# Packing the own tiles of exponents in a sparse-attention layer

## The chip, the cores and the metric

The kernel runs on one core of a Trainium2 chip. The metric is the device time of one execution in microseconds (us); the median of three runs before the change is 1934.23 us. About 0.2% (3.9 us) is what a measurement of this kernel can tell from no change.

## The reference

Two layers act on 1024 tokens of width 1024. Layer 0 mixes with gated linear attention, layer 1 with sparse attention of 16 heads: an indexer scores all earlier keys, the 256 best are kept for each query, and softmax runs over these. The change touches layer 1 alone. What is computed there, for one head:

```
logits = einsum('bthd,btjd->bthj', q_b, k_sel) * ATTN_SCALE
logits = where(valid, logits, -inf)          # valid: idx <= t_pos
probs  = softmax(logits)                     # over the selected keys
o      = einsum('bthj,btjd->bthd', probs, v_sel)
out    = (o * silu(z)) @ w_out
```

The kernel does not gather: it adds a bias to the scores of all earlier keys, which hides those that were not selected, takes exponents, and multiplies by all values of earlier keys. One key and one value serve all 16 heads.

## The kernel before, in words

Layer 1 is done in two halves of 512 queries. Half 0 has four tiles of 128 keys, half 1 eight: four "past" ones, which every query may see, and four "own" ones, of which query tile t sees the first t+1. Ten of the sixteen own pairs of key tile and query tile are thus unmasked or on the diagonal, and six are empty.

For one head h of a half (function `attend`):

- `A(t)` (four steps, one for each query tile): TensorE (PE) forms the scores into tile `S`; VectorE (DVE) adds the bias, scales, and takes the row minimum `mx` (L1592, tile `P`); then `exp` on ScalarE (ACT, L1599) writes exponents to `sq` with one instruction and the row sum to `sm`; then `turned` (L1605) turns every 32x32 square of `sq` in place on DVE.
- `store` (L1618): four DMAs for each group of four key tiles write `sq` to a scratch tensor `sqd` in DRAM, with all sixteen places of key tile and query tile. Half 1 has two such groups: group 0 holds the past keys, group 1 the own keys. `load` (L1628) reads a group back with keys on the partitions: tile `PT`, 1 MB. In this text PT0 is the tile of group 0 and PT1 that of group 1. Half 0 has group 0 alone, in two buffers; half 1 has one buffer each for PT0 and PT1.
- `parts` (L1645 on ACT, L1643 on DVE) splits each key tile of `PT` into a high part `ph` and a low part, which takes the place in `PT`. `pv` multiplies by the values: three matmuls (L58, tile `o`) for each key tile, of which the third reads the low part; the last own key tile is used whole.
- `inverse` and `to_all` turn the row sums into a factor for the output, by way of a small DRAM row (`row`, then `inv`).

There is one buffer `sq` for all heads. So `exp` of the next head waits until the stores of this one have landed, and the store waits for the last `turned`.

The order of work on each engine is written by the program, with a clock of its own (`Flow.now`) that counts matmul columns alone. A step is put on a heap with a due time (`fl.at`) and is emitted when the clock has passed it and its conditions (`fl.req`) hold. Engines then run their lists in that order, each waiting for what it needs. All DMAs of this stage but the small `row` ones are issued from the SP queue, in order, and SP waits at a DMA whose inputs or buffers are not ready: those behind it wait too. Beside stores and loads these are the weights (`whi` and `wlo`, L174, 512 KB each).

Around the heads runs a fixed plan (`slots`): while one head's exponents are made, the head before is multiplied, and matmul units of projections (tile `pb`) fill the rest. Heads 0 to 3 have two units each; from head 4 on a slot has three. The emptied `P` buffers, `ph` (three) and the PSUM tiles bound how far ahead engines may run.

Of the kernel before, what the change touches and what calls it, by code (L numbers as in the profile page):

```python
# [10 lines left out]
F32 = mybir.dt.float32  # L11
# [12 lines left out]
HT = 512  # L24
# [253 lines left out]
def trunk_kernel(ctx, tc, x_tok, x_T, p_T, pos, freq, g_q, g_k, g_v, g_z, g_a, g_a2, g_ba, g_gn, g_o,  # L278
# [1276 lines left out]
    def attend(st, h, half, ap, sq):  # L1555
# [15 lines left out]
        def A(t):  # L1571
            def f():
                T = base + t
                n = 128 * T + 128
                (qh, ql), = get(("q", h))
                i = t % (half + 2)
                last = max(range(i, 4, half + 2))
                fl.req(("P", h, t - half - 2) in st if t != i else h == 0 or ("P", h - 1, last) in st)
                st["A", h] = t
                ts_ = slice(t * 128, t * 128 + 128)  # L1580
                P = ap.tile([128, 128 * (base + last) + 128], F32, tag=f"P{i}", name="P")[:, :n]
                if t == 0:
                    st["sm", h] = cp.tile([128, 4], F32, tag=("ss", "rs")[h % 2], name="sm", bufs=2)
                    st["mx", h] = cp.tile([128, 3, 8], F32, tag="mid", name="mx", bufs=2)
                sm, mx = st["sm", h], st["mx", h][:, 0, t:t + 1]
                lim = 3.0e38
                for a, e in cuts(n):
                    e2 = max(e, 256)
                    ps = spsum()
                    for i, (l, r) in enumerate(((qh, kT[0]), (qh, kT[1]), (ql, kT[0]))):  # L1590
                        mm(ps[:, :e2], l[:, ts_], r[:, a:a + e2], i == 0, i == 2)
                    dve.tensor_tensor_reduce(P[:, a:a + e], ps[:, :e], bias_t[T][:, a:a + e], op0=OP.add, op1=OP.min,  # L1592
                                             scale=-ATTN_SCALE, scalar=lim, accum_out=mx)
                    lim = mx

                def exp():
                    fl.req(st["x"] == nb * h)
                    to, rows = by_key[:, t, :n // 128], P.rearrange("p (j b r) -> p j b r", b=4, r=32)
                    act.activation(to, rows, AF.Exp, scale=-1.0, bias=mx, accum_out=sm[:, t:t + 1])  # L1599
                    st["P", h, t] = True  # L1600
                    after(0.4 + n / 1000.0, turned)

                def turned():
                    x = squares[:, t, :, :n // 128]
                    dve.transpose(x, x)  # L1605
                    st["D", h, t] = True
                after(0.9, exp)
            return f

        def store(i):  # L1610

            def f():
                get(*(("D", h, t) for t in range(4)))
                fl.req(st["x"] == nb * h + i)
                dt = st["dram", h, i] = dp.tile([4, 32, 4, HT], F32, tag=f"sq{i}", name="sqd", bufs=2)
                sq4 = sq.rearrange("p (b i c) -> p i b c", b=4, i=nb)
                for a in range(4):
                    nc.sync.dma_start(dt[:, :, a].rearrange("b p c -> p b c"), sq4[32 * a:32 * a + 32, i])  # L1618
                st["x"] += 1
            return f  # L1620

        def load(i):

            def f():
                dt, _ = get(("dram", h, i), ("dram", h, nb - 1))
                fl.req(st["pv"] >= (h * G - (0 if i else G - 4) if half else (h - 1) * G))
                PT = ap.tile([128, 4, HT], F32R, tag=f"PT{i}", name="PT", bufs=2 - half)
                nc.sync.dma_start(PT.bitcast(F32), dt.rearrange("b p a c -> (b p) a c"))  # L1628
                st["PT", h, i] = PT
            return f  # L1630

        def parts(g):
            def f():
                j, t0 = groups[g]
                PT, = get(("PT", h, j // 4))
                fl.req(st["sp"] - st["pv"] < 3)
                st["sp"] += 1
                lo = PT.rearrange("p a (j c) -> p j a c", c=128)[:, j % 4, :, 32 * t0:]
                ph = ap.tile([128, HT], F32R, tag="ph", name="ph", bufs=3)
                hi = ph[:, :HT - 128 * t0].rearrange("p (a c) -> p a c", a=4)  # L1640

                def second():
                    dve.tensor_sub(lo, lo.bitcast(F32), hi.bitcast(F32))  # L1643
                    st["parts", h, g] = hi, lo
                chain((0, lambda: act.activation(hi, lo.bitcast(F32), AF.Copy)), (0.8, second))  # L1645
            return f
# [39 lines left out]
        def pv(g):  # L1686
            first, last = g == 0, g == len(groups) - 1

            def f():
                (ph, pl), = get(("parts", h, g))  # L1690
                fl.req(not first or st.get("done", -1) == h - 1, not last or h < 5 or st["out"] >= h - 4)
                st["pv"] += 1
                if first:
                    st["o", h] = pp.tile([128, HT], F32, tag="o", name="o")
                o = st["o", h]
                o3 = o.rearrange("p (a c) -> p a c", c=128)
                j, t0 = groups[g]
                if last:
                    PT, = get(("PT", h, half))
                    whole = PT.bitcast(F32).rearrange("p a (j c) -> p j a c", c=128)[:, 3, :, 96:]  # L1700
                    mm(o3[:, :, 96:], vT[0][:, base + 3].bitcast(F32), whole, False, False)
                for i, (l, r) in enumerate(((vT[0], ph), (vT[1], ph), (vT[0], pl))):
                    mm(o3[:, :, 32 * t0:], l[:, j], r, first and i == 0, last and i == 2)
# [19 lines left out]

        n = range(len(groups))
        return [fl.ordered(x) for x in ([A(t) for t in range(4)], [parts(g) for g in n], [pv(g) for g in n],
                                     [store(i) for i in range(nb)], [load(i) for i in range(nb)], [inverse, to_all])]

    def dsa_out(st, js, ch, y, norm=None, ahead=1):
        fl.need(lambda: st.get("y") == NK)
# [86 lines left out]
    for half in range(NH):  # L1816
# [4 lines left out]
            nc.sync.dma_start(vT[0][:, 3].bitcast(F32), kv_s[4, :, 384:512])  # L1821
            nc.sync.dma_start(vT[0][:, 7].bitcast(F32), vf_s[1])
        fl.run(*(unit(u) for u in first_units))
        sq = ap.tile([128, (4 * half + 4) * HT], F32, name="sq")
        pool.memset(sq, 0.0)
        st["x"] = st["sp"] = st["pv"] = st["out"] = 0
        core = 8.6 if half else 3.6
        plan = list(slots())
# [1 line left out]
        for h, units in enumerate(plan, -1):  # L1830
# [5 lines left out]
            if h >= 0:  # L1836
# [16 lines left out]
            if h < 15:  # L1853
# [117 lines left out]
```

## Time and profile before

| what | value |
|---|---|
| runs, us | 1932.59, 1935.04, 1934.23; median 1934.23 |
| the profiled execution, us | 1935.94, with a span of 1934.2 |
| granted TensorE clock | 1.00 |
| PE, DVE, ACT busy | 99%, 77%, 52% of the span |
| half 0 of layer 1's heads | about 1070 to 1400 us of the span |
| half 1 of layer 1's heads | about 1470 to 1865 us |
| SP store and load issues | `sqd<-sq` 192 of 256 KB, `PT<-sqd` 48 of 1024 KB |

Times in the trace count from the span's start. A row of a timeline gives start, duration, engine, line, operation, output and input, shape, count, and in brackets how long the engine had been idle and what ended that. A row of the chain of waits gives start, duration and what ran. The stretches of a window table give, for each engine, the busy time and (x) the instructions, then the clock, the share of the DMA engines that was busy and GB/s. In DMA rows "SPq" is the SP queue issuing; its duration is that of issuing, not of the transfer.

### The profile page before, as it was taken

The numbers are of one execution on the slowest core, as the hardware profiler recorded it, in microseconds if no ns is written. First come the engines' busy times: TensorE is split into PE (matmuls) and PEld (weight loads), VectorE is DVE, ScalarE is ACT, GpSimd is POOL, SyncE is SP. The second block draws the span as 40 slices with busy tenths as digits, with TensorE's granted clock in tenths as the row PEclk, the third lists the DMA queues.
The fourth block names the chain that finished last, engine by engine and source line by source line (L and its number), as shares of the span: only waits on it lengthen the run. The fifth ranks groups of instructions, "written<-read, shape, count | busy, mean of one in ns | idle before, by whom it ended". The sixth has DMA issues, their size and how long they took to land.

```text
span 1934.2 us, 26875 instructions
## 1 busy us (share of the span) xinstructions
PE 1914.7 (99%) x8826; PEld 1590.6 (82%) x8826; DVE 1495.4 (77%) x3081; ACT 1002.4 (52%) x1896; POOL 153.0 (8%) x301
## 2 busy tenths in 40 slices
PE   9999999999999999999999999999999999999999
PEld 7888888888888888888888888888888778888887
DVE  5777666696778888878858987778798887777873
ACT  5564636445564646464535676756443443434432
POOL 0000000010010101010101001221001010000000
PEclk9999999999999999999999999999999999999999
DMA  4567766768667767677688588987877898888874
GB/s 156 207 218 230 225 220 215 225 207 274 223 221 262 244 224 247 222 242 228 211 287 302 169 294 288 318 293 283 305 247 283 324 305 302 299 303 289 290 285 142
DMA packets 200764, 488.91 MB, mean 253 GB/s; under 512 B 26504, under 2 KB 42928, under 8 KB 194480
## 3 DMA queue, kind: packets, MB, share of 16 engines
q1 hardware_dynamic: 193200, 474.55, 72.1%
q0 software_dynamic: 7424, 12.64, 2.0%
q8 instruction: 69, 1.13, 0.2%
q14 instruction: 71, 0.58, 0.1%
HBM read 343.18 MB, written 143.92 MB: 252 GB/s over the span
## 4 chain that ended last, share of the span: by engine, by line
PE 88%; DVE 5%; ACT 3%; DMA 2%; issue 1%; SPq 0%; DVEq 0%; ACTq 0%
PE pb L58 67%; PE o L58 8%; PE U L58 6%; PE S L58 5%; DMA PT<-sqd 1%; PE tr L58 1%; DVE sq L1605 1%; DVE PT L1643 0%; DMA wst<-in_g_v 0%; DVE sc L1141 0%; PE xt L62 0%; DVE wlo L191 0%; PE ix L58 0%; SPq L1618 0%; PE S L62 0%
## 5 line engine op out<-in xcount | busy, mean ns | idle before, releaser
L58 PE MATMUL pb<-x,whi 128*128 128x512 f32 x2272 | 704.2, 391 | 0.8 <-DVE x L411 0.7
L58 PEld LDWEIGHTS pb<-x,whi 128*128 128x128 f32 x2272 | 419.5, 188 | 80.0 <-DVE x L411 1.9
L58 PE MATMUL pb<-x,wlo 128*128 128x512 f32 x1136 | 442.6, 390 | 0.0
L58 PE MATMUL pb<-whi,u 128*128 128x512 f32 x1024 | 339.5, 392 | 1.5 <-ACT u L419 0.8
L58 PEld LDWEIGHTS pb<-x,wlo 128*128 128x128 f32 x1136 | 213.2, 188 | 45.8 <-DVE wlo L191 0.4
L58 PEld LDWEIGHTS pb<-whi,u 128*128 128x128 f32 x1024 | 192.2, 188 | 41.3 <-ACT u L419 1.2
L58 PE MATMUL pb<-wlo,u 128*128 128x512 f32 x512 | 199.6, 390 | 0.0
L191 DVE TENSOR_TENSOR wlo<-wst,whi 128x512 fp32r<-128x512 f32 x232 | 154.5, 683 | 35.1 <-ACT whi L189 34.9
L189 ACT ACTIVATE whi<-wst 128x512 fp32r<-128x512 f32 x232 | 136.4, 622 | 73.9 <-DMA wst<-in_g_k 28.8
L1599 ACT ACTIVATE sq<-P,mx 128x128 f32<-128x128 f32 (+7 forms) x128 | 98.8, 772 | 87.6 <-DVE mx L1592 58.0
L58 PE MATMUL S<-kT,q 128*128 128x512 f32 (+2 forms) x576 | 123.6, 343 | 1.7 <-DVE q L411 1.2
L1645 ACT ACTIVATE ph<-PT 128x512 fp32r<-128x512 f32 (+2 forms) x160 | 86.2, 558 | 63.0 <-PE o L58 43.4
L58 PEld LDWEIGHTS S<-kT,q 128*128 128x128 f32 x576 | 100.4, 188 | 20.5 <-DVE mx L1592 2.1
L58 PEld LDWEIGHTS pb<-wlo,u 128*128 128x128 f32 x512 | 96.2, 188 | 18.2
L1643 DVE TENSOR_TENSOR PT<-PT,ph 128x512 fp32r<-128x512 f32 (+2 forms) x160 | 92.6, 592 | 21.4 <-ACT ph L1645 21.2
L1207 ACT ACTIVATE tk<-sc,tki 128x768 f16<-128x768 f32 (+2 forms) x90 | 92.9, 1033 | 25.4 <-DVE tki L1216 21.6
L1605 DVE STREAM_TRANSPOSE sq<-sq 128x128 f32<-128x128 f32 (+7 forms) x128 | 97.7, 768 | 2.0 <-ACT sq L1599 2.0
L237 DVE TENSOR_TENSOR pst<-pst,phi 128x512 fp32r<-128x512 f32 x130 | 88.7, 682 | 7.4 <-ACT phi L233 7.4
L753 ACT ACTIVATE junk<-o 128x512 bf16<-128x512 f32 x32 | 19.1, 597 | 139.7 <-DVE ot L748 116.6
L58 PE MATMUL o<-ph,vT 128*128 128x512 f32 (+2 forms) x320 | 90.8, 365 | 0.0
L58 PE MATMUL pb<-whi,x 128*128 128x512 f32 x256 | 85.3, 392 | 0.0
L58 PE MATMUL U<-whi,x 128*128 128x512 f32 x256 | 84.6, 389 | 0.0
(330 smaller groups left out, 3400.4 us busy)
## 6 DMA issues: line engine op xcount, KB each, us to landing
whi<-whs SPq DMA_DIRECT2D x128, 512.0 KB, 6.1
wlo<-wls SPq DMA_DIRECT2D x128, 512.0 KB, 6.7
sqd<-sq SPq DMA_DIRECT2D x192, 256.0 KB, 4.4
PT<-sqd SPq DMA_DIRECT2D x48, 1024.0 KB, 7.7
whs<-phi SPq DMA_DIRECT2D x130, 256.0 KB, 4.1
wls<-pst SPq DMA_DIRECT2D x130, 256.0 KB, 4.1
wst<-in_g_z SPq DMA_DIRECT2D x32, 512.0 KB, 4.7
wst<-in_g_o SPq DMA_DIRECT2D x32, 512.0 KB, 5.1
```

Source lines behind the costliest of these rows:

```text
L58: self.pe.matmul(out, lhsT, rhs, start=start, stop=stop)
L189: self.nc.scalar.activation(hi[:, c], st[:, c], AF.Copy, scale=1.0 if gain is None else gain)
L191: self.nc.vector.tensor_sub(lo[:, c], st[:, c], hi[:, c].bitcast(F32))
L237: self.nc.vector.tensor_sub(st, st.bitcast(F32), hi.bitcast(F32))
L753: act.activation(junk, ps, AF.Square, accum_out=u["ss"][:, c:c + 1])
L1207: act.activation(junk()[:, :n], scs[j], AF.Sign, bias=cand[:, j:j + 1].bitcast(F32), accum_out=cnt[:, j:j + 1])
L1599: act.activation(to, rows, AF.Exp, scale=-1.0, bias=mx, accum_out=sm[:, t:t + 1])
L1605: dve.transpose(x, x)
L1643: dve.tensor_sub(lo, lo.bitcast(F32), hi.bitcast(F32))
L1645: chain((0, lambda: act.activation(hi, lo.bitcast(F32), AF.Copy)), (0.8, second))
```

## The change

- `exp` writes own key tiles to ten packed cells of 32 columns (times four for the key's quarter) and past key tiles to a separate region. So one instruction becomes one to three: for half 0 five a head where there were four, for half 1 nine.
- `turned` turns whole packed regions: in half 0 after query tiles 2 and 3; in half 1 the past region after tiles 1 and 3, half of it each time, the own region after 2 and 3.
- Own stores carry 320 columns, where they carried 512 (160 KB for 256 KB a DMA), and own loads 640 KB where they were 1024 KB. Past ones stay.
- In half 1, PT1 (own) has two buffers and is loaded as soon as it is stored, ahead of PT0 in the list of loads; it used to be loaded after the previous head's multiplication had ended.
- `sq` shrinks and is no longer zeroed (POOL's memset goes); row sums go to a wider tile, and one or two small additions bring the pieces of a sum together.
- `parts` and `pv` address the own tiles as runs of 32 columns. Matmul count, order and sizes stay.

```diff
+        cells = ((0, 1, 0),), ((0, 2, 2),), ((0, 2, 4), (2, 3, 1)), ((0, 4, 6),)
                 def exp():
-                    to, rows = by_key[:, t, :n // 128], P.rearrange("p (j b r) -> p j b r", b=4, r=32)
-                    act.activation(to, rows, AF.Exp, scale=-1.0, bias=mx, accum_out=sm[:, t:t + 1])
+                    rows = P.rearrange("p (j b r) -> p j b r", b=4, r=32)
+                    to = [(cell[:, c:c + e - j], rows[:, base + j:base + e], 8 if j else 0) for j, e, c in cells[t]]
+                    if half:
+                        to.append((past[:, t], rows[:, 0:base], 4))
+                    for x, r, i in to:
+                        act.activation(x, r, AF.Exp, scale=-1.0, bias=mx, accum_out=sm[:, i + t:i + t + 1])
                 def turned():
-                    x = squares[:, t, :, :n // 128]
-                    dve.transpose(x, x)
+                    get(*(("P", h, i) for i in range(t)))
+                    if half and t % 2:
+                        x = by_b[:, :, 0:HT].rearrange("p b (j x) -> p b j x", j=4)[..., 32 * t - 32:32 * t + 32]
+                        dve.transpose(x, x)
+                    if t > 1:
+                        x = by_b[:, :, HT * half:][:, :, 192 * (t - 2):192 + 128 * (t - 2)]
+                        dve.transpose(x, x)
...
+                n = HT if i < half else 320
+                dt = st["dram", h, i] = dp.tile([4, 32, 4, n], F32, tag=f"sq{n}", name="sqd", bufs=2)
...
-                fl.req(st["pv"] >= (h * G - (0 if i else G - 4) if half else (h - 1) * G))
-                PT = ap.tile([128, 4, HT], F32R, tag=f"PT{i}", name="PT", bufs=2 - half)
+                fl.req(st["pv"] >= (h * G - G + 4 if i < half else (h - 1) * G))
+                if i < half:
+                    PT = ap.tile([128, 4, HT], F32R, tag="PT0", name="PT")
+                elif half:
+                    PT = ap.tile([128, 4, 320], F32R, tag="PT1", name="PT", bufs=2)
...
+            if half:
+                dve.tensor_add(sm[:, 0:4], sm[:, 0:4], sm[:, 4:8])
+            dve.tensor_add(sm[:, 2:3], sm[:, 2:3], sm[:, 10:11])
...
-                                     [store(i) for i in range(nb)], [load(i) for i in range(nb)], [inverse, to_all])]
+                                     [store(i) for i in range(nb)], [load(i) for i in reversed(range(nb))],
...
-        sq = ap.tile([128, (4 * half + 4) * HT], F32, name="sq")
-        pool.memset(sq, 0.0)
+        sq = ap.tile([128, 4 * (HT * half + 320)], F32, name="sq")
...
-                    fl.at(start + 1.5, loads[1])
...
-                    fl.at(start + (max(dur - 1.0, 18.0) if h >= 0 else 16.0), loads[0])
+                    fl.at(start + (16.5 if h >= 0 else 15.0), loads[0])
+                    fl.at(start + (max(dur - 1.0, 18.0) if h >= 0 else 16.0), loads[1])
```

In the program after the change `loads[0]` is the load of PT1 and `loads[1]` that of PT0.

The SP queue of half 1 at the stores and loads of head 1, and the stores of head 2 with their loads, before (512 columns are a full group; `128x2048` is a whole PT tile):

```order
L1618 DMA sqd<-sq 32x4x512 x8
L1628 DMA PT<-sqd 128x2048 x2
L1676 DMA row<-uf 4x128
L174 DMA whi<-whs 128x1024
L174 DMA wlo<-wls 128x1024
L1684 DMA inv<-row 128x512
L1618 DMA sqd<-sq 32x4x512 x8
L174 DMA whi<-whs 128x1024
L174 DMA wlo<-wls 128x1024
L1628 DMA PT<-sqd 128x2048
```

The same place after the change (`128x1280` is the packed PT1):

```order
L1629 DMA sqd<-sq 32x4x512 x4
L1629 DMA sqd<-sq 32x4x320 x4
L1646 DMA PT<-sqd 128x1280
L1646 DMA PT<-sqd 128x2048
L1704 DMA row<-uf 4x128
L174 DMA whi<-whs 128x1024
L174 DMA wlo<-wls 128x1024
L1712 DMA inv<-row 128x512
L1629 DMA sqd<-sq 32x4x512 x4
L1629 DMA sqd<-sq 32x4x320 x4
L174 DMA whi<-whs 128x1024
L174 DMA wlo<-wls 128x1024
```

PT1 now stands between the last own store, whose data it reads, and PT0; before, PT0 came directly behind the stores (or behind the weights that follow them), and PT1 after it.

The DVE list of half 1 from the last transpose ahead of head 2's first split on, before (`PT<-PT,ph` is the split's second step for one key tile; the last transpose, `128x32x32`, is the one that the stores wait for):

```order
L1605 STREAM_TRANSPOSE sq<-sq 128x4x6x32
L1643 TENSOR_TENSOR PT<-PT,ph 128x4x128
L411 TENSOR_TENSOR q<-qf,q 128x512
L1605 STREAM_TRANSPOSE sq<-sq 128x4x7x32
L1643 TENSOR_TENSOR PT<-PT,ph 128x4x128
L1605 STREAM_TRANSPOSE sq<-sq 128x32x32
L1643 TENSOR_TENSOR PT<-PT,ph 128x4x128
L1528 SCALAR_TENSOR_TENSOR z<-z,pb 128x512
L1659 RECIPROCAL inverse_10144<-sm 128x4
```

The same place after the change:

```order
L1613 STREAM_TRANSPOSE sq<-sq 128x4x4x64
L1666 TENSOR_TENSOR PT<-PT,ph 128x4x128
L411 TENSOR_TENSOR q<-qf,q 128x512
L1616 STREAM_TRANSPOSE sq<-sq 128x4x192
L1666 TENSOR_TENSOR PT<-PT,ph 128x4x128
L1613 STREAM_TRANSPOSE sq<-sq 128x4x4x64
L1616 STREAM_TRANSPOSE sq<-sq 128x4x128
L1666 TENSOR_TENSOR PT<-PT,ph 128x4x128
L1528 SCALAR_TENSOR_TENSOR z<-z,pb 128x512
L1679 TENSOR_TENSOR mx<-mx 128x4
L1680 TENSOR_TENSOR mx<-mx 128x1
L1687 RECIPROCAL inverse_10144<-mx 128x4
```

After the first split there stood transposes of 896 and 1024 elements a row; now there are 768, 1024 (the past stores wait for this one) and 512 (the own stores). Two small additions stand ahead of the reciprocal.

More of the change, by code (lines that the diff above doesn't have):

```diff
@@ L1563, in attend @@
         G, nb = len(groups), half + 1
-        by_key = sq.rearrange("p (b j t r) -> p t j b r", b=4, t=4, r=32)
-        squares = sq.rearrange("p (b j t r) -> p t b j r", b=4, t=4, r=32)
+        by_b = sq.rearrange("p (b c) -> p b c", b=4)
+        past = by_b[:, :, 0:HT].rearrange("p b (j t r) -> p t j b r", t=4, r=32) if half else None
+        cell = by_b[:, :, HT * half:].rearrange("p b (c r) -> p c b r", r=32)
+        cells = ((0, 1, 0),), ((0, 2, 2),), ((0, 2, 4), (2, 3, 1)), ((0, 4, 6),)
         def get(*keys):
@@ L1582, in f @@
                 if t == 0:
-                    st["sm", h] = cp.tile([128, 4], F32, tag=("ss", "rs")[h % 2], name="sm", bufs=2)
                     st["mx", h] = cp.tile([128, 3, 8], F32, tag="mid", name="mx", bufs=2)
+                    st["sm", h] = st["mx", h].rearrange("p a b -> p (a b)")[:, 8:]
                 sm, mx = st["sm", h], st["mx", h][:, 0, t:t + 1]
@@ L1614, in f @@
                 fl.req(st["x"] == nb * h + i)
-                dt = st["dram", h, i] = dp.tile([4, 32, 4, HT], F32, tag=f"sq{i}", name="sqd", bufs=2)
-                sq4 = sq.rearrange("p (b i c) -> p i b c", b=4, i=nb)
+                n = HT if i < half else 320
+                dt = st["dram", h, i] = dp.tile([4, 32, 4, n], F32, tag=f"sq{n}", name="sqd", bufs=2)
                 for a in range(4):
-                    nc.sync.dma_start(dt[:, :, a].rearrange("b p c -> p b c"), sq4[32 * a:32 * a + 32, i])
+                    nc.sync.dma_start(dt[:, :, a].rearrange("b p c -> p b c"),
+                                      by_b[32 * a:32 * a + 32, :, HT * i:HT * i + n])
                 st["x"] += 1
@@ L1625, in f @@
                 dt, _ = get(("dram", h, i), ("dram", h, nb - 1))
-                fl.req(st["pv"] >= (h * G - (0 if i else G - 4) if half else (h - 1) * G))
-                PT = ap.tile([128, 4, HT], F32R, tag=f"PT{i}", name="PT", bufs=2 - half)
+                fl.req(st["pv"] >= (h * G - G + 4 if i < half else (h - 1) * G))
[3 more added lines that the diff above has]
+                    PT = ap.tile([128, 4, 320], F32R, tag="PT1", name="PT", bufs=2)
+                else:
+                    PT = ap.tile([128, 4, HT], F32R, tag="PT0", name="PT", bufs=2)
+                    PT = PT.rearrange("p a c -> p (a c)")[:, :1280].rearrange("p (a c) -> p a c", a=4)
                 nc.sync.dma_start(PT.bitcast(F32), dt.rearrange("b p a c -> (b p) a c"))
@@ L1637, in f @@
                 st["sp"] += 1
-                lo = PT.rearrange("p a (j c) -> p j a c", c=128)[:, j % 4, :, 32 * t0:]
                 ph = ap.tile([128, HT], F32R, tag="ph", name="ph", bufs=3)
                 hi = ph[:, :HT - 128 * t0].rearrange("p (a c) -> p a c", a=4)
+                if j < base:
+                    lo = PT.rearrange("p a (j c) -> p j a c", c=128)[:, j]
+                else:
+                    at, end, step = ((0, 7, 2), (3, 8, 2), (1, 9, 7))[t0]
+                    lo = PT.rearrange("p a (c r) -> p a c r", r=32)[:, :, at:end:step]
+                    hi = hi.rearrange("p a (t r) -> p a t r", r=32)
                 def second():
@@ L1653, in inverse @@
             row = st["row", h] = dp.tile([4, 128], F32, tag="row", name="row", bufs=2)
+            sm = st["sm", h]
+            if half:
+                dve.tensor_add(sm[:, 0:4], sm[:, 0:4], sm[:, 4:8])
+            dve.tensor_add(sm[:, 2:3], sm[:, 2:3], sm[:, 10:11])
+            st["sm", h] = sm[:, 0:4]
             if in_turn:
@@ L1699, in f @@
                     PT, = get(("PT", h, half))
-                    whole = PT.bitcast(F32).rearrange("p a (j c) -> p j a c", c=128)[:, 3, :, 96:]
+                    whole = PT.bitcast(F32)[:, :, 288:]
                     mm(o3[:, :, 96:], vT[0][:, base + 3].bitcast(F32), whole, False, False)
+                to = o3[:, :, 32 * t0:]
+                if j >= base:
+                    to = to.rearrange("p a (t r) -> p a t r", r=32)
                 for i, (l, r) in enumerate(((vT[0], ph), (vT[1], ph), (vT[0], pl))):
-                    mm(o3[:, :, 32 * t0:], l[:, j], r, first and i == 0, last and i == 2)
+                    mm(to, l[:, j], r, first and i == 0, last and i == 2)
                 if g == len(groups) - 2:
@@ L1725, in attend @@
         return [fl.ordered(x) for x in ([A(t) for t in range(4)], [parts(g) for g in n], [pv(g) for g in n],
-                                     [store(i) for i in range(nb)], [load(i) for i in range(nb)], [inverse, to_all])]
+                                     [store(i) for i in range(nb)], [load(i) for i in reversed(range(nb))],
+                                     [inverse, to_all])]
     def dsa_out(st, js, ch, y, norm=None, ahead=1):
```

## The prediction

> **What bounds the kernel now.** I read the page's busy shares first, then busy time by stretches, the chain of waits, and the SP and ACT timelines of the stretch where PE idles.
>
> ```profile
> PE 1914.7 (99%) x8826; PEld 1590.6 (82%) x8826; DVE 1495.4 (77%) x3081; ACT 1002.4 (52%) x1896; POOL 153.0 (8%) x301
> ```
>
> PE is busy 1914.7 of 1934.2 us, and the order list of PE is the same before and after: same matmuls, same sequence, same sizes. The change can therefore move the time only through PE's waits, of which there are 19.5 us in all, so I looked for those in layer 1's heads. Stretches of half 1, one head's stores to the next one's, heads 1 to 6 (PE, PEld, DVE, ACT, POOL busy, clock, DMA share, GB/s):
>
> ```profile
> 1501.00:1523.00 22.00, 21.48 (x102) 17.35 (x101) 20.46 (x43) 11.61 (x23) 0.00 (x0) 1.00 0.86 327
> 1523.00:1545.00 22.00, 21.47 (x102) 17.56 (x101) 17.48 (x39) 9.48 (x18) 2.02 (x4) 1.00 0.91 306
> 1545.00:1566.00 21.00, 19.93 (x93) 16.00 (x91) 18.88 (x41) 10.54 (x20) 1.97 (x4) 1.00 0.90 306
> 1566.00:1588.00 22.00, 21.80 (x102) 18.22 (x103) 17.61 (x39) 9.48 (x18) 1.99 (x4) 1.00 0.93 316
> 1588.00:1613.00 25.00, 23.25 (x108) 19.04 (x108) 21.41 (x45) 8.40 (x16) 1.97 (x4) 1.00 0.84 290
> 1613.00:1639.00 26.00, 26.00 (x123) 21.82 (x123) 18.78 (x41) 10.24 (x19) 1.99 (x4) 1.00 0.95 325
> ```
>
> The first five lack 0.52 + 0.53 + 1.07 + 0.20 + 1.75 = 4.07 us of PE; the sixth, a slot with three units, lacks nothing although DMA is busiest there. So from head 6 on PE sets the pace, and something else does in heads 0 to 4. The chain of waits says what (start, duration, what ran):
>
> ```profile
> 1532.18 8.35 DMA PT<-sqd
> 1540.55 0.64 ACT ph L1645
> ...
> 1544.03 1.24 DVE sq L1605
> ```
>
> It is a loop: PT0 of head 2 lands, ACT makes `ph` from it, the last exponents of head 3 follow on ACT, DVE turns them, and SP starts head 3's stores. Behind these comes the next PT0 (SP timeline; `x8` are eight stores, `x2` PT0 and PT1):
>
> ```profile
> 1522.57 7.42 SPq L1618 DMA_DIRECT2D sqd<-sq  x8
> ...
> 1545.33 7.48 SPq L1618 DMA_DIRECT2D sqd<-sq  x8
> 1553.12 3.29 SPq L1628 DMA_DIRECT2D PT<-sqd  x2
> ...
> 1565.59 7.14 SPq L1618 DMA_DIRECT2D sqd<-sq  x8
> ...
> 1588.22 6.39 SPq L1618 DMA_DIRECT2D sqd<-sq  x8
> ```
>
> One turn takes 22.76 us (1522.57 to 1545.33), 20.26 and 22.63. PE's work for a turn, from the stretches, is 21.5, 19.9 and 21.8: the loop is a little longer than PE's work each time, and what lengthens it is paid by PE. ACT shows its two waits, for the stores to leave `sq` and for PT0:
>
> ```profile
> 1545.62 0.63 ACT L1645 ACTIVATE ph<-PT 128x512 fp32r<-128x512 f32 x1 [1.26 <-DMA PT<-sqd]
> ...
> 1556.33 0.83 ACT L1599 ACTIVATE sq<-P,mx 128x640 f32<-128x640 f32 x1 [7.10 <-DMA sqd<-sq]
> ...
> 1560.07 0.63 ACT L1645 ACTIVATE ph<-PT 128x512 fp32r<-128x512 f32 x1 [0.35 <-DMA PT<-sqd]
> ```
>
> At head 3 the stores have landed at 1556.3, PT0 at 1560.07, the next stores go 5.5 us later, and `sq`'s exponents in between have filled ACT with less than 4 us. So the term that counts is when PT0 lands.
>
> **The change part by part.** *1. PT0's landing.* It now stands behind smaller stores, but behind PT1 too, and PT1 cannot be issued until the last own store has landed. What the DMA engines moved while stores ran out (1553 to 1556) and while PT0 ran (1556 to 1560):
>
> ```profile
> 1553.00:1556.00 3.00, 3.00 (x17) 2.62 (x16) 2.42 (x8) 0.00 (x0) 0.00 (x0) 1.00 0.94 229
> 1556.00:1560.00 4.00, 4.00 (x20) 3.28 (x19) 2.67 (x7) 3.39 (x7) 0.00 (x0) 1.00 1.00 367
> ```
>
> Stores shed 4 x 96 KB = 393,216 B a head: at 229 GB/s 1.72 us. No row shows DMAs with runs of 1280 B; the bounds are 0 (a run costs what it did at 2 KB) and 1.72, and I take 1.72, as all rows here move faster or at that rate (at 367 GB/s it would be 1.07). PT1 ahead of PT0 is 655,360 B at 367 GB/s: 1.79 us. Before, PT0 was queued while own stores still ran, so the engines never emptied. Now SP sits at PT1 until these stores are down, and PT0, the `row`, the weights and `inv` stand behind it in SP's queue. How long from an issue to bytes when the engines are not fed, half 0 shows:
>
> ```profile
> 1149.52 0.34 SPq L1628 DMA_DIRECT2D PT<-sqd  x1
> ...
> 1150.00:1151.00 1.00, 1.00 (x6) 0.82 (x5) 0.98 (x4) 1.00 (x3) 0.00 (x0) 1.00 0.84 139
> 1151.00:1152.00 1.00, 1.00 (x6) 0.82 (x5) 1.00 (x4) 1.00 (x4) 0.00 (x0) 1.00 0.58 205
> 1152.00:1153.00 1.00, 1.00 (x6) 0.83 (x5) 1.00 (x3) 1.00 (x3) 0.00 (x0) 1.00 1.04 442
> ```
>
> Full rate comes 2.5 us after the issue. If the bytes of the two slow stretches were PT's own, 139/442 + 205/442 = 0.77 us of it was not lost, leaving 1.7; if half were, 2.1. I take 1.9 with bounds 0 (other transfers fill the gap) and 2.5. Heads 0 and 3, whose loads stand right behind the stores: -1.72 + 1.79 + 1.9 = +1.97 each. Head 1: there PT0's issue waited for its buffer until 1510.59, 2.4 us after the stores' issues ended, while PT1 now has a second buffer and may use that time; between 0.1 and 1.97, taken as 1.0. Heads 2 and 4: 1 MB of weights lies between stores and loads and covers the gap, so -1.72 + 1.79 = +0.07 each; without that cover it would be the 1.97. Sum **+5.1**. With all bounds at once it would be -1.4 (no gap, head 1's PT1 wholly within the wait for PT0's buffer: 4 x 0.07 - 1.72) to +16.5 (nothing shed, a gap of 2.5 in three heads: 5 x 1.79 + 3 x 2.5).
>
> [...]
>
> *2. DVE between PT0 and the stores.* Groups of instructions with shapes apart (busy, mean ns | idle before):
>
> ```profile
> L1605 DVE STREAM_TRANSPOSE sq<-sq 128x896 f32<-128x896 f32 x16 | 17.6, 1101 | 0.0
> ...
> L1605 DVE STREAM_TRANSPOSE sq<-sq 128x768 f32<-128x768 f32 x16 | 15.6, 973 | 0.0
> ...
> L1605 DVE STREAM_TRANSPOSE sq<-sq 128x512 f32<-128x512 f32 x16 | 11.3, 705 | 1.2 <-ACT sq L1599 1.2
> ```
>
> Behind the landing the order lists show transposes of 896 and 1024 elements before; now 768 and 1024 stand ahead of the first, past stores: 973 for 1101 ns, **-0.6** over five turns. *3.* The own 512 (0.7 us) and small additions (I estimate 0.3 us; the shortest DVE rows are a tenth of a microsecond) come after it: own stores are issued last, so the transpose ends while SP is still at the past ones, but splits of PT's next key tiles wait behind it. That is a shift by 0.7 + 0.3 - 0.13, once and not per turn: **+0.9**.
>
> *4. Slack.* The DVE and PE timelines of head 0's splits:
>
> ```profile
> 1502.35 0.67 DVE L1643 TENSOR_TENSOR PT<-PT,ph 128x512 fp32r<-128x512 f32 x1
> ```
>
> ```profile
> 1503.57 0.39 PE L58 MATMUL o<-PT,vT 128*128 128x512 f32 x1
> ```
>
> DVE takes up its next row at 1502.95, and PE's use of the low part starts at 1503.57: 0.6 us are free before PE waits, **-0.6**. *5. PT1 earlier.* ACT's wait of 1.26 us for PT1 at 1545.62 goes; it delayed splits that PE waited for by 0.5 (the stretch's 0.53): **-0.5**.
>
> *6. The last two heads.* There ACT waits for loads that follow the stores directly:
>
> ```profile
> 1832.66 1.15 ACT L1645 ACTIVATE ph<-PT 128x512 fp32r<-128x512 f32 x2 [1.56 <-DMA PT<-sqd]
> ...
> 1852.44 1.68 ACT L1645 ACTIVATE ph<-PT 128x512 fp32r<-128x512 f32 x3 [5.70 <-DMA PT<-sqd]
> ```
>
> ```profile
> 1854.55 2.20 PE o L58 x9
> ```
>
> The second row's `ph` is made two microseconds before PE's use of it in the chain of waits, and DVE has the splits of three key tiles to do in them. A gap of 1.9 less 1.0 of smaller transfers (393,216 B at 367 GB/s), charged in full: **+0.9** (0 to 2). *7. Half 0.*
>
> ```profile
> L1599 ACT ACTIVATE sq<-P,mx 128x384 f32<-128x384 f32 x16 | 9.8, 614 | 9.2 <-DVE mx L1592 9.1
> ...
> L1599 ACT ACTIVATE sq<-P,mx 128x256 f32<-128x256 f32 x16 | 8.0, 499 | 1.9 <-DVE mx L1592 1.9
> ```
>
> ```profile
> 1070.00:1400.00 330.00, 326.44 (x1537) 273.12 (x1536) 267.12 (x682) 206.09 (x459) 40.91 (x78) 1.00 0.81 281
> ```
>
> ```profile
> 1175.82 0.50 PE L58 MATMUL o<-PT,vT 128*128 128x512 f32 x1 [1.61 <-DVE PT L1643]
> ```
>
> One exponent of 384 columns becomes two, of 256 and 128: 499 ns and, 115 ns less for each 128 by these two rows, an estimated 384, for 614. That is +0.3 on ACT for each head, with ACT busy 206 of 330 us; it counts once, where PE waited 1.61 us for a split: **+0.3**. The stores shrink by 37%, which could take back up to that 1.61, but PE idles only 3.6 us in the 330, and the other two are at other places.
>
> Nothing is charged for: the added exponents of half 1 (nine for four, 1.4 to 1.9 us more ACT a head), since ACT is busy 8.4 to 11.6 of 21 to 25 us and idles 7.10 at the place where they start, and starts earlier as stores land earlier (without that cover, they would add their length to the loop); the low parts in runs of 32 columns, as the 384-column matmul that now reads `PT` with gaps takes what one from a contiguous tile takes; POOL's two memsets, for which nobody waits; the weights behind the loads, used by the next slot; and anything from head 6 to 13, where PE lacked 0.00.
>
> ```profile
> L58 PE MATMUL S<-kT,q 128*128 128x384 f32 x144 | 33.2, 338 | 0.0
> ...
> L58 PE MATMUL o<-PT,vT 128*128 128x384 f32 x32 | 10.8, 339 | 0.0
> ```
>
> (In the second, `PT` is read in four runs of 96 columns; in the first, a tile without gaps.)
>
> **Sum:** 5.1 - 0.6 + 0.9 - 0.6 - 0.5 + 0.9 + 0.3 = +5.5 us. On the profiled execution (span 1934.2, 1935.94 in all) that is 1941.4; it lay 1.7 above the median of the runs, so on 1934.23 it is **1939.7 us**.
>
> **The rivals.** *No difference.* The gap is filled: other weights are under way when SP sits at PT1, or receipt is quick (0.5 for 1.9). Then term 1 is 0.57 + 0.57 + 0.3 + 0.14 = 1.6, term 6 is 0, the others -0.5 together, and the sum +1.1: **1935.3**. For it: DMA is 84 to 95% busy, so some transfer is mostly there. Against: all of them go through the one SP queue that waits.
>
> *Faster.* What binds is not PT0 but `sq`'s release and the late PT1. The waits between 1480 and 1600 us (total, times, longest):
>
> ```profile
> ACT sq L1599 <- DMA sqd<-sq: 15.8, 3, 7.1
> ACT ph L1645 <- DMA PT<-sqd: 9.3, 5, 3.4
> ```
>
> The wait for the stores is the bigger; if the earlier landing (1.72 us) pulls exponents and with them the next stores ahead, the loop falls below PE's work, and PE gains its 4.07 us and 0.5 at the place of term 6: **1929.7**. It decides if PT0 lands no later than now. Against: after the stores' landing ACT still waits for PT0, at each of the heads shown.
>
> *Slower by more.* Runs of 1280 B cost what runs of 2 KB did, so stores shed nothing: term 1 grows by 1.72 in five heads, 8.6 us: **1948.3**. It decides from the stores' packets on: if a 320-column store takes the time of a 512-column one. For it: stores move 229 GB/s where loads move 367, so something other than bytes costs there.
>
> **How the numbers follow.** Forecast (1936 to 1943) 0.50, no difference 0.28, faster 0.14, slower by more 0.08. What a measurement can tell from no change is 0.2%, 3.9 us: 1930.4 to 1938.1. Of the forecast 0.03 lies below 1938.1, of the faster case 0.02 above 1930.4. Faster: 0.12; same: 0.28 + 0.03 + 0.02 = 0.33; slower: 0.47 + 0.08 = 0.55. The range leaves out most of the faster and of the slowest case: 1932 to 1946.
>
> **What would show it.** Term 1: in the SP timeline a step between the last own store and PT1's issue, and bytes about 2 us after it; from stores to PT0's landing 17 us in head 3 instead of 14.7 (1545.33 to 1560.07); distances from stores to stores of 22 to 24 us; PE idle of about 9 us for 4.07 between 1500 and 1615. Term 2 and 3: transposes of 768 and 512 after PT0's `ph`. Term 5: no ACT wait for PT1. Term 6: a longer wait at the last head. Wrong it would be if PT0 lands within 15 us of the stores' start, if stores of 320 columns last as long as those of 512, or if PE idles after head 6.

## The result and the profile after

| | before | after |
|---|---|---|
| median of five runs, us | 1935.04 (1932.59 to 1936.91) | 1945.97 (1943.97 to 1950.03) |
| ratio, 95% interval | | 1.0055 (1.0044 to 1.0067) |
| profiled execution: span, PE busy, us | 1934.2, 1914.7 | 1948.2, 1919.9 |

The change made the kernel 10.9 us slower. The forecast was +5.5: the sign and the range (up to 1946) held, the size was half of what came. Where the time went is another matter: most of it went to places for which the forecast had charged nothing.

The profiled execution is the slowest of the five. PE idled 1948.2 - 1919.9 = 28.3 us in it, 8.8 more than before, and was busy 5.2 us longer, 3.4 of them by a halved clock (last section). Busy time by stretches of half 1 (columns as in the prediction), heads 0 to 5, then the stretch in which head 8 begins to be multiplied, then head 12:

```profile
1501.00:1620.00 119.00, 115.56 (x535) 94.49 (x534) 103.81 (x227) 61.07 (x154) 8.71 (x18) 1.00 0.81 271
1690.00:1710.00 20.00, 17.50 (x81) 14.17 (x80) 15.04 (x28) 6.29 (x14) 1.97 (x4) 1.00 0.83 275
1790.00:1815.00 25.00, 22.68 (x104) 18.41 (x103) 19.71 (x42) 9.79 (x25) 1.99 (x4) 1.00 0.89 297
```

In heads 0 to 5, where the forecast put 5 us, PE lacks 3.44 us, less than the 4.07 of before. At heads 8 and 12, where it put nothing, PE lacks 2.50 and 2.32. Before the change it lacked nothing there:

```profile
1690.00:1710.00 20.00, 20.00 (x95) 16.66 (x95) 16.41 (x38) 7.19 (x14) 1.98 (x4) 1.00 0.94 309
1790.00:1815.00 25.00, 25.00 (x118) 20.88 (x117) 21.41 (x44) 9.68 (x19) 1.99 (x4) 1.00 0.92 315
```

PE's waits in the timeline (in brackets the idle time and what ended it):

```profile
1177.13 0.51 PE L58 MATMUL o<-PT,vT 128*128 128x512 f32 x1 [1.92 <-DVE PT L1666]
...
1699.39 0.50 PE L58 MATMUL o<-PT,vT 128*128 128x512 f32 x1 [1.07 <-DVE PT L1666]
...
1702.48 0.50 PE L58 MATMUL o<-PT,vT 128*128 128x512 f32 x1 [1.43 <-DVE PT L1666]
...
1804.30 0.50 PE L58 MATMUL o<-PT,vT 128*128 128x512 f32 x1 [0.89 <-DVE PT L1666]
...
1807.38 0.50 PE L58 MATMUL o<-PT,vT 128*128 128x512 f32 x1 [1.43 <-DVE PT L1666]
...
1866.22 0.73 PE L58 MATMUL o<-ph,vT 128*128 128x512 f32 x2 [2.13 <-ACT ph L1668]
```

The first is half 0's wait (1.61 before), then head 8, head 12 and the last head, which had none. PE's list is the same in both kernels, so the start of the same PE instruction in the two traces tells how late the changed kernel is at each place:

| place (time before) | late by, us | what lies between |
|---|---|---|
| 1175.8, half 0's wait ends | 1.3 | 0.4 stood before half 0; 0.6 at a wait for a reciprocal (1115.1, see runs 2 and 3), 0.3 at this wait |
| 1197.1 | 3.0 | 1.7: a halved clock, see the last section |
| 1468.5, half 1 begins | 4.1 | small steps |
| 1590.7, head 4 | 3.6 | heads 0 to 4: -0.5 |
| 1651.4 | 4.1 | |
| 1695.9, head 8 | 6.6 | +2.5 |
| 1796.5 to 1797.9, head 12 | 7.8 to 9.4 | +2.3 |
| 1854.4, last head | 11.8 | +2.1 |
| 1857.1 | 13.8 | another halved clock, 1.7 |
| end | 14.1 | |

The steps that term 1 was built on are all to be seen at head 3. SP's queue of the changed kernel (`x2` is now PT1, then PT0):

```profile
1549.00 6.01 SPq L1629 DMA_DIRECT2D sqd<-sq  x8
1558.05 0.84 SPq L1646 DMA_DIRECT2D PT<-sqd  x2
```

The DMA engines meanwhile (the last two columns are their busy share and GB/s):

```profile
1557.00:1558.00 1.00, 1.00 (x7) 0.82 (x6) 0.69 (x3) 0.00 (x0) 0.00 (x0) 1.00 0.05 18
1558.00:1559.00 1.00, 1.00 (x8) 0.87 (x7) 0.81 (x3) 0.99 (x3) 0.00 (x0) 1.00 0.00 0
1559.00:1560.00 1.00, 1.00 (x7) 0.91 (x6) 1.00 (x4) 1.00 (x4) 0.00 (x0) 1.00 0.94 220
1560.00:1564.00 4.00, 4.00 (x20) 3.27 (x19) 3.71 (x10) 2.63 (x10) 0.00 (x0) 1.00 1.00 404
```

And ACT, when PT0 has landed:

```profile
1564.39 0.63 ACT L1668 ACTIVATE ph<-PT 128x512 fp32r<-128x512 f32 x1 [1.30 <-DMA PT<-sqd]
```

The stores are issued by 1555.0, SP then sits for 3.0 us, and from 1557 to 1559 the DMA engines do next to nothing (busy shares of 0.05 and 0.00). PT0 lands 15.4 us after the stores' start, for 14.7 before: +0.65, not +1.97. A part of the difference is that the two loads ran at 404 GB/s where the prediction used 367 (4.2 us for 4.6, worked out from their bytes); that PT0 before had PT1 issued right behind it, and so beside it, may be another, which no run tests. The next stores then start 4.6 us after that (1568.99), for 5.5 before. One turn takes 19.99 us, for 20.26.

At head 7, whose PT0 decides when head 8 can be multiplied, the order is another. SP's queue before:

```profile
1676.48 0.38 SPq L1628 DMA_DIRECT2D PT<-sqd  x1
```

and after, from the own stores on:

```profile
1674.19 2.35 SPq L1629 DMA_DIRECT2D sqd<-sq  x4
1681.43 0.34 SPq L1646 DMA_DIRECT2D PT<-sqd  x1
1681.86 0.38 SPq L174 DMA_DIRECT2D whi<-whs  x1
1682.34 0.38 SPq L174 DMA_DIRECT2D wlo<-wls  x1
1682.81 0.73 SPq L1646 DMA_DIRECT2D PT<-sqd  x1
```

SP sits 4.9 us (1676.5 to 1681.4), longer than at head 3; here weights stand among the stores, and the own stores land later. PT0 is issued with PT1 and 1 MB of weights ahead of it. ACT's first `ph`, before:

```profile
1684.66 0.62 ACT L1645 ACTIVATE ph<-PT 128x512 fp32r<-128x512 f32 x1
```

and after:

```profile
1691.63 0.63 ACT L1668 ACTIVATE ph<-PT 128x512 fp32r<-128x512 f32 x1 [2.27 <-DMA PT<-sqd]
```

That is 7.0 us later by the clock, some 3 more than the 3.8 to 4.1 that the kernel was late by at this place; PE then waits 2.5. So PE had only some 0.4 to 0.7 us to spare here, though it had not idled at all before.

### The profile page after: what moved, and what is told of

It is laid out like the page before. It is cut to its first block, busy times and chain, and to the rows that moved or that the text cites. A ratio compares the mean times of both kernels' runs of the same rounds, so it can differ in the third digit from the quotient of the medians.

```text
span 1948.2 us, 27094 instructions
## 1 busy us (share of the span) xinstructions
PE 1919.9 (99%) x8826; PEld 1592.4 (82%) x8826; DVE 1502.1 (77%) x3097; ACT 1028.4 (53%) x2088; POOL 147.4 (8%) x299
## 4 chain that ended last, share of the span: by engine, by line
PE 82%; DVE 8%; DMA 6%; ACT 2%; issue 1%; SPq 0%; ACTq 0%; DVEq 0%
PE pb L58 63%; PE o L58 7%; PE U L58 6%; PE S L58 4%; DMA wlo<-wls 2%; DMA PT<-sqd 1%; DMA sqd<-sq 1%; DVE PT L1666 1%; PE tr L58 1%; DVE sq L1616 1%; DVE sc L1141 1%; DVE tk L1163 1%; DMA whi<-whs 0%; DMA wst<-in_g_v 0%; DVE tk L1230 0%
## 5 line engine op out<-in xcount | busy, mean ns | idle before, releaser
L1605 ACT ACTIVATE sq<-P,mx 128x512 f32<-128x512 f32 (+2 forms) x224 | 125.4, 561 | 73.6 <-DVE mx L1594 66.0
L1594 DVE CUSTOM_DVE_ANT_0 P<-S,bias 128x512 f32<-128x512 f32 (+3 forms) x128 | 71.6, 566 | 17.1 <-PE S L58 14.9
```

The lines of the kernel that those rows point to most:

```text
L1605: act.activation(x, r, AF.Exp, scale=-1.0, bias=mx, accum_out=sm[:, i + t:i + t + 1])
```

## The experiments

Two theories: **O**, the order of loads costs (SP sits at PT1 until the own stores have landed, with PT0 behind it), and **P**, packing itself costs (more ACT instructions, a longer DVE list ahead of the splits). All ratios are against the kernel before, run on the same chip beside it.

**1. Packed, loads as before.**

```diff
-                                     [store(i) for i in range(nb)], [load(i) for i in reversed(range(nb))],
+                                     [store(i) for i in range(nb)], [load(i) for i in range(nb)],
...
+                    fl.at(start + 1.5, loads[1])
...
-                    fl.at(start + (16.5 if h >= 0 else 15.0), loads[0])
-                    fl.at(start + (max(dur - 1.0, 18.0) if h >= 0 else 16.0), loads[1])
+                    fl.at(start + (max(dur - 1.0, 18.0) if h >= 0 else 16.0), loads[0])
```

> Packing as in the change, but PT0 is again first in the list of loads and due when it was, and PT1 (packed, two buffers) is due 1.5 us into the next slot. Theory O (the order of loads costs: SP sits at PT1 until the own stores have landed, and PT0 is behind it): the waits for the split at heads 8 and 12 (2.3 to 2.5 us each) and at head 15 (2.1 us) are gone, and of the +10.9 us only half 0's part is left: 1935 to 1938 us. Theory P (packing itself costs, by more ACT instructions and a longer DVE list ahead of the split): the same waits stay, 1943 to 1947 us.

Measured: 1934.41 us, ratio 0.9994 (0.9985 to 1.0003), the kernel before 1936.41. The loss is gone, and theory P falls; the time is even a little below theory O's range. What PE waited for between 1480 and 1870 us, with the total, the times and the longest, first before:

```profile
PE o L58 <- DVE PT L1643: 3.5, 5, 1.0
```

after the change:

```profile
PE o L58 <- DVE PT L1666: 8.3, 11, 1.4
PE o L58 <- ACT ph L1668: 2.1, 1, 2.1
```

and in this run:

```profile
PE o L58 <- DVE PT L1666: 1.2, 3, 0.4
```

So with the old order packing costs little, and it shortens the loop of heads 0 to 4. What it does cost in half 1 stands at heads 8 and 12, with 0.4 us each: the last exponents ahead of head 7's first `ph` are three instructions where there was one, and keep ACT busy for 1.6 us (1683.65 to 1685.23) where it was 1.0. Busy time from 1480 to 1600 us in this run:

```profile
1480.00:1600.00 120.00, 119.36 (x556) 98.70 (x555) 104.34 (x227) 60.78 (x154) 7.97 (x16) 1.00 0.87 286
```

PE lacks 0.64 us, where it lacked 4.07. How much of that is packing, one trace does not tell: in run 2, whose half 1 is that of before, PE lacks 2.13 us in this stretch, and in run 8, whose half 1 is also that of before, 3.78.

```profile
1480.00:1600.00 120.00, 117.87 (x550) 96.72 (x549) 100.00 (x210) 51.36 (x100) 7.98 (x16) 1.00 0.94 325
```

So packing gives heads 0 to 4 between 1.5 and 3.4 us. ACT's waits of this stretch fit that. Before there stood 15.8 us of `sq` waiting for `sqd` (the prediction's rival, "faster"). After the change:

```profile
ACT sq L1605 <- DMA sqd<-sq: 7.2, 2, 4.1
```

In this run there is no such row; ACT's waits for exponents are put down to `mx` (19.9 us in 10 waits). That is not to say that the stores never bind: at head 3 ACT starts at 1557.19, and SP issues PT1, which waits for the same landing, at 1557.16, so `mx` and the landing came within some 0.1 us. That earlier landing is what shortens the loop is read from these rows; no run tests it alone.

**2. and 3. Each half alone.** The packed `attend`, `sq` and dues are used in one half, those of before in the other:

```diff
-        S = [attend(st, h, half, ap, sq) for h in range(16)]
+        S = [(attend_packed if half == 0 else attend_full)(st, h, half, ap, sq) for h in range(16)]
```

> Half 0 packed as in the change, half 1 as before the change. In the trace half 0 lost about 0.3 us at one wait (1.92 for 1.61 us), 1.7 us by a halved clock right behind it, and 1.1 us in small steps. If these are of the change: 1936 to 1938 us. If the small steps and the halved clock are noise of the one execution: 1934 to 1936 us, as before.

> Half 1 packed and its loads reordered as in the change, half 0 as before the change. Both theories put the larger part here: heads 8, 12 and 15 with 2.4 us each and 1.7 us of halved clock after the last: 1942 to 1945 us. If it is below 1939 us, half 0 carries more than the trace showed.

Measured: half 0 alone 1936.98 us, ratio 1.0001 (0.9992 to 1.0010); half 1 alone 1945.74 us (a little above its range), ratio 1.0048 (1.0036 to 1.0061). All of the loss that the times show is half 1's. (1936.98 lies in the range of the first expectation, but against a kernel before that took 1936.41, so the time does not decide between the two.) In half 0 PE's wait grew as in the changed kernel:

```profile
1176.88 0.51 PE L58 MATMUL o<-PT,vT 128*128 128x512 f32 x1 [1.92 <-DVE PT L1666]
```

but no halved clock followed (a matmul of 512 columns behind it takes 0.39 to 0.40 us, in the changed kernel 0.63). The small steps are there again. From the same PE instruction to the same (1068 to 1468.5 by the times of before) half 0 takes 400.4 us before, 400.6 and 400.2 where it is not packed (runs 3 and 7), but 401.7 and 402.1 in the packed ones whose clock did not fall (runs 2 and 5, mean clock 1.000), and 403.3 to 404.1 in those whose clock did (mean 0.998 and 0.999). So packing costs half 0 some 1.3 us and more, beside the clock. The 0.3 above is one part; another is a wait for the reciprocal of the row sums, ahead of which one of the small additions now stands. It is 0.7 us in all six traces of a packed half 0, here the changed kernel's, and in none of the others:

```profile
1115.14 0.27 PE L62 MATMUL S<-ident,mx 128*4 128x128 f32 x1 [0.68 <-DVE mx L1683]
```

**4. PT0 first, PT1 right behind it.** Only the list's order is turned back; the due times of the change stay, with the earlier one now PT0's.

```diff
-                                     [store(i) for i in range(nb)], [load(i) for i in reversed(range(nb))],
+                                     [store(i) for i in range(nb)], [load(i) for i in range(nb)],
```

> Packing as in the change, PT0 first, PT1 due right behind it (not in the next slot). Theory O: PT0 is issued as soon as the past stores have landed, so the waits at heads 8, 12 and 15 go as in the run with the loads as before: 1935 to 1938 us. If PT1's bytes beside PT0 are what delays it and not the wait on SP, PT0 still lands late: 1940 to 1944 us.

Measured: 1936.76 us, ratio 1.0003 (0.9994 to 1.0011). PT1's bytes behind PT0 do no harm to it (though in the last slot PE waits 1.95 us for a weight, which the other traces do not show). Theory O has the cause: what stands ahead of PT0.

What stands ahead of it is three things: the wait for the own stores, PT1's 640 KB, and at heads 7 and 11 weights of 1 MB. Two runs tell them apart.

**5. The wait alone.** As run 4, with a load of 128 B from the own scratch tensor ahead of PT0, so that SP waits there as the changed kernel does, while PT1 stays behind PT0:

```diff
+                if half and i == 0:
+                    seen = cp.tile([1, 4, 8], F32, tag="seen", name="seen")
+                    nc.sync.dma_start(seen, st["dram", h, 1][0, 0:1, :, 0:8])
                 nc.sync.dma_start(PT.bitcast(F32), dt.rearrange("b p a c -> (b p) a c"))
```

> As the run with PT0 first and PT1 right behind it, but with a load of 128 B from the own scratch tensor ahead of PT0 on SP, so that PT0 is issued only when the own stores have landed, while PT1's bytes stay behind it. If the wait is what costs: PT0 lands 2 to 5 us later at heads 7 and 11, heads 8 and 12 wait again for the split, 1940 to 1945 us. If PT1's 640 KB ahead of PT0 are what costs: 1936 to 1939 us. If half and half: 1938 to 1941 us.

Measured: 1940.64 us, ratio 1.0023 (1.0014 to 1.0032), in the range of "half and half" and at the lower end of that for the wait. SP's queue at head 7:

```profile
1673.31 0.67 SPq L174 DMA_DIRECT2D whi<-whs  x1
1674.08 0.79 SPq L174 DMA_DIRECT2D wlo<-wls  x1
1677.66 0.57 SPq L1648 DMA_DIRECT2D seen<-sqd  x1
1678.33 0.87 SPq L1649 DMA_DIRECT2D PT<-sqd  x2
```

The wait is there (to 1677.7), but the weights run in its gap and PT0 is next. Heads 8 and 12 do not wait more than in run 4; heads 0 to 4 do (1.84 us of PE idle, table below), and so does the last head:

```profile
1857.21 0.73 PE L58 MATMUL o<-ph,vT 128*128 128x512 f32 x2 [1.09 <-ACT ph L1671]
```

**6. Weights ahead of the wait.** The changed kernel, but PT1 may be issued only when PT0's condition holds, so that the weights of heads 7 and 11 get ahead of both:

```diff
-                fl.req(st["pv"] >= (h * G - G + 4 if i < half else (h - 1) * G))
+                fl.req(st["pv"] >= (h * G - G + 4 if half else (h - 1) * G))
```

> The changed kernel, but PT1 may be issued only when the condition that PT0 has (the past key tiles of the head before are used up) holds too, so that the weights that stood between PT1 and PT0 at heads 7 and 11 now stand ahead of SP's wait and run in its gap. PT1 still stands right ahead of PT0, behind the own stores' landing. If the weights behind the wait make heads 8 and 12 late (1 MB at some 400 GB/s is 2.6 us, the waits there are 2.3 to 2.5 us): these waits go, the last head and heads 0 to 4 stay as in the changed kernel, 1939 to 1942 us where before is 1936. If PT1's own bytes make them late: the waits stay, 1944 to 1947 us.

Measured: 1944.10 us, ratio 1.0040 (1.0027 to 1.0054): the time is that of the second expectation, but the waits are those of neither. The order came as meant (SP's queue at head 7):

```profile
1675.78 0.89 SPq L174 DMA_DIRECT2D whi<-whs  x1
1676.76 0.72 SPq L174 DMA_DIRECT2D wlo<-wls  x1
1680.55 0.80 SPq L1646 DMA_DIRECT2D PT<-sqd  x2
```

and the waits at heads 8 and 12 shrank, but did not go:

```profile
1700.63 0.50 PE L58 MATMUL o<-PT,vT 128*128 128x512 f32 x1 [1.43 <-DVE PT L1666]
...
1803.62 0.50 PE L58 MATMUL o<-PT,vT 128*128 128x512 f32 x1 [0.67 <-DVE PT L1666]
```

The runs form a ladder (PE's idle time by stretches of each profiled execution, in us; the last head is the sum of PE's waits as its multiplication begins):

| ahead of PT0 | ratio | heads 0 to 4 | head 8 | head 12 | last head |
|---|---|---|---|---|---|
| before the change | 1 | 4.07 | 0.00 | 0.00 | 0.00 |
| half 1 as before (run 2) | 1.0001 | 2.13 | 0.00 | 0.00 | 0.36 |
| nothing, PT1 late (run 1) | 0.9994 | 0.64 | 0.39 | 0.39 | 0.00 |
| nothing, PT1 behind (run 4) | 1.0003 | 0.62 | 0.42 | 0.39 | 0.00 |
| the wait (run 5) | 1.0023 | 1.84 | 0.42 | 0.41 | 1.55 |
| wait and PT1 (run 6) | 1.0040 | 3.93 | 1.43 | 0.67 | 2.34 |
| wait, PT1, weights (the change) | 1.0055 | 3.44 | 2.50 | 2.32 | 2.37 |
| wait, PT1, weights (run 3) | 1.0048 | 3.63 | 1.81 | 2.83 | 2.44 |

Of the 4.8 us at heads 8 and 12 together (4.6 in run 3), 0.8 is packing's, which run 1 has too; the wait alone adds nothing, PT1's bytes 1.3 and the weights 2.5 to 2.7. One head alone cannot be split so: with the same order run 3 has 0.7 less at head 8 than the change and 0.5 more at head 12. Ratios of neighbouring steps from run 5 on overlap in their intervals; the columns show which waits make each step.

**7. Half 1 packed with the loads as before, half 0 not packed.** Run 1 with half 0 left as it was.

> Half 1 packed with PT0 first and PT1 due in the next slot, as in the run with the loads as before; half 0 as before the change. In that run's trace heads 0 to 4 of half 1 gained about 4 us, and half 0 had lost 3 to 4 by then (1.7 of them a halved clock). If half 0's loss is of packing it: this one is 2 to 4 us faster than before, 1932 to 1934 us where before is 1936. If the loss was noise of the one execution, it is as before: 1935 to 1937 us.

Measured: 1933.91 us against 1936.12, ratio 0.9988 (0.9979 to 0.9997). This is faster than the kernel before by 0.12%, within the 0.2% that a measurement can tell from no change, though the interval leaves out 1. In the trace these are the 3.4 us of heads 0 to 4, less 0.45 and 0.72 us of PE idle at heads 8 and 12. The first expectation came: without half 0's packing the kernel gains twice as much as run 1 (0.06%), as the steps in half 0 of runs 2 and 3 would have it. Its busy time from 1480 to 1600 us:

```profile
1480.00:1600.00 120.00, 119.39 (x560) 98.92 (x559) 103.65 (x230) 60.92 (x155) 7.94 (x16) 1.00 0.87 290
```

**8. A longer wait in half 0**, in the kernel before, to see whether the halved clock follows from it:

```diff
                 def second():
+                    if half == 0 and h == 4 and g == 0:
+                        spare = tmp1()
+                        for _ in range(2):
+                            dve.tensor_sub(spare, hi.bitcast(F32), hi.bitcast(F32))
                     dve.tensor_sub(lo, lo.bitcast(F32), hi.bitcast(F32))
```

> The kernel before, with two DVE subtractions of 512 columns (0.6 us each) into an unused tile ahead of the split that PE waits for at 1175.8 us. The wait grows from 1.6 to 2.8 us. If a wait of about 1.9 us and more makes the granted clock fall: 0.5 for 3.4 us right after it, so that 1.7 us are lost beside the 1.2, and the time after this place is 2.9 us later. If the dips seen so far have nothing to do with PE's waits: 1.2 us and a clock of 1.00.

Measured: one execution, 1938.19 us. The wait came out as meant, and the clock stayed at 1.00:

```profile
1177.79 0.50 PE L58 MATMUL o<-PT,vT 128*128 128x512 f32 x1 [2.92 <-DVE PT L1647]
```

```profile
1179.00:1181.00 2.00, 2.00 (x10) 1.65 (x10) 2.00 (x5) 2.00 (x4) 0.00 (x0) 1.00 0.69 152
```

The length of the wait alone does not decide; the last section takes this up.

## Why the prediction was right or wrong

**The forecast, slower because PT0 stands behind a wait and behind PT1: right in mechanism.** Runs 1 and 4 take the order back and the loss is gone; runs 5 and 6 put wait, PT1 and weights back one by one. The gap is as large as said: 2 us at head 3 with DMA shares of 0.05 and 0.00, for 1.9. (The last bytes of the stores move by 1557.6, 0.4 us before ACT and SP go on at 1558.0; the first bytes of PT1 move at 1559.0, 0.95 us after its issue.) Stores landed earlier too, by 2.0 us for 1.72 at head 3: by ACT's row they had landed 11.0 us after their start before (1545.33 to 1556.33), and now have in 9.0:

```profile
1558.01 0.40 ACT L1605 ACTIVATE sq<-P,mx 128x128 f32<-128x128 f32 x1 [4.12 <-DMA sqd<-sq]
```

Part of these 2.0 us is that PT0 no longer runs beside the last stores: in run 1, where it does, they land 10.5 us after their start here (1546.67 to 1557.16, SP's issue of PT1). Over all 192 stores the median from issue to landing fell from 4.4 to 3.4 us in the change. So the slowest rival, that 320-column stores cost what 512-column ones do, did not come: their issue at head 3 takes 6.0 us for 7.5. Of the signs that the prediction named for term 1 the step in SP's queue came; PT0's landing 17 us after the stores' start and PE idle of 9 us did not (15.4 and 3.4), and turns of 22 to 24 us were 20 to 22.4, no longer than before.

**Term 1, +5.1 in heads 0 to 4: mis-sized, and met by a gain that was not counted.** The order costs these heads 2.8 us (3.44 in the change against 0.64 in run 1). Against it stands what packing gives there, 1.5 to 3.4 us (2.13 to 4.07 with the old stores, 0.64 in run 1). One reading in the term was wrong: at head 1 PT0's issue at 1510.59 did not wait for its buffer, as the term has it, but for the stores' landing, to which SP's waits of that stretch are put down (4.3 us in three, the longest 2.3). PT1, whose stores land later still (SP issued it at 1513.13 before), could not use that time. The prediction gave the packing only terms 2 and 5 (-1.1) and put the rest with a rival at 0.14: that `sq`'s release binds, worth "its 4.07 us". By the rows of run 1 that rival had hold of something, in a loop with two limits close together, and only the order hid it. The argument against it, that ACT still waits for PT0 after the stores have landed, was not enough: behind PT0's landing at head 3 DVE had three transposes to do ahead of the next stores, which took 5.5 us, and in the change it has two, in 4.6.

**"Anything from head 6 to 13" at nothing: the step that failed.** It read slack from PE's idle time of 0.00. That says only that nothing was late, not how much later it may come. At head 7 ACT took PT0 without a wait and PE did not idle, yet the room was some 0.4 to 0.7 us: a `ph` some 3 us later cost 2.5. Two such heads are 4.8 us. And at these heads the weights stand between PT1 and PT0, an order that the prediction, which worked out heads 0 to 4 and the last two, did not look for. It had itself named PE idling after head 6 as a sign of being wrong, and that sign came.

**Term 6, +0.9 at the last head: mechanism right, size 2.4.** The term charged the gap less smaller transfers. The wait alone cost 1.55 here (run 5), more than that, and PT1's bytes ahead of PT0, which the term left out, 0.8 (run 6).

**Term 7, +0.3 in half 0: right at its place** (1.61 to 1.92), but packing costs half 0 1.3 us and more in the traces. The small additions were charged in half 1 alone, and in half 0 PE waits 0.7 us behind one. In the times of run 2 this cannot be told from no change. **Term 5**: ACT's wait for PT1 is gone, but PE still waits 1.1 us at that head's last splits (0.79 and 0.32 us, at 1550.76 and 1552.06), so its 0.5 us cannot be seen. **Nothing for the added exponents**: not quite, they cost 0.4 us each at heads 8 and 12. Nothing for 32-column runs and memsets fits run 1.

So +5.5 and +10.9 share their cause, but not their places: 2.8 for 5.1 in the early heads with 1.5 to 3.4 back, 4.8 for 0 in the middle, 2.4 for 0.9 at the end, and in four of the five runs, by their mean clock, a fall of the clock (1.7 us each in the trace), which no term had. That the sum came out slower and just inside the range is in good part luck: with packing's gain the largest term came to about nothing, and heads that were charged nothing took its place. The bound of 0.2% puts the result outside "no change", as the forecast's 0.55 for slower had it.

## What to carry to other kernels

On an in-order DMA queue, ask of each transfer that is moved ahead what it waits for: the wait is paid by everything behind it, also if the transfer is small (128 B in run 5, where the time grew by 0.2%), and weights that slip behind the wait are paid for too (2.5 to 2.7 us at heads 8 and 12). An engine that never idled has shown that nothing was late, not that there is room (before the change PE idled 0.00 us at head 8 and had some 0.4 to 0.7 to spare); measure the room as the time between a landing and its use, at each kind of place and not at the first ones only. When one change holds a saving and a reordering, try each alone: here the saving was worth about 0.1% at most and the reordering cost five times that. And take a second trace of unchanged code before a gain is read from one: here PE idled 2.1, 3.8 and 4.1 us in the same heads 0 to 4 of three traces.

## What the hardware showed beside

In the changed kernel the granted clock fell to half right behind two of PE's waits. After the wait that ended at 1177.13 (1.92 us) the clock column reads:

```profile
1178.00:1179.00 1.00, 1.00 (x5) 0.82 (x4) 1.00 (x3) 0.75 (x1) 0.00 (x0) 0.72 0.46 102
1179.00:1180.00 1.00, 1.00 (x3) 0.78 (x3) 1.00 (x3) 1.00 (x4) 0.00 (x0) 0.50 0.95 389
1180.00:1181.00 1.00, 1.00 (x4) 0.74 (x3) 0.74 (x2) 1.00 (x3) 0.43 (x1) 0.50 0.40 164
1181.00:1182.00 1.00, 1.00 (x5) 0.81 (x4) 0.00 (x0) 0.95 (x2) 1.00 (x3) 0.58 0.26 66
...
1867.00:1868.00 1.00, 0.91 (x3) 0.43 (x3) 1.00 (x2) 0.73 (x2) 0.00 (x0) 0.96 1.01 121
```

It is 0.50 for 3.4 us, so 1.7 us are lost, nearly as much as in the wait itself. The five runs of the change fit that: the one whose mean clock was 1.000 took 1943.97 us, three at 0.999 took 1945.45 to 1947.12, and the one at 0.998, with two such falls in its trace, 1950.03.

Of nine waits of PE of 1.9 us or longer in layer 1 the clock fell behind six: 1.92 and 2.13 us in the change, 1.90 in run 1, 1.90 and 1.95 in run 4, 2.11 in run 6. (In runs 1, 4 and 6 the matmuls tell it: one of 512 columns takes 0.63 us soon after these waits, for 0.39 to 0.40 at the full clock.) Behind 1.92 us in run 2, 1.97 in run 3 and 2.92 in run 8 it did not fall, nor behind the 1.61 of before or the waits of 1.43 in the change.

So the length of a wait alone does not decide, and what does is not shown. By the clock column of the change the two falls begin at 1178.43 and 1867.92 us and last 3.41 us each; a third, behind PE's last work, begins at 1946.43. They lie 689.49 and 78.51 us apart, which is 202 and 23 times 3.413. In the 3.41 us ahead of the first two falls PE idled 1.92 and 1.72 us.
